# RWKV stage of a decoder trunk: block transposes on VectorE in place of DMAs through DRAM, mixes and masks on GpSimd, another order

## The chip, the cores and the metric

The kernel runs on one core of a Trainium2 chip. The metric is the device time of one execution in microseconds. The figure for the kernel before is the median of three runs. One further execution is recorded by the hardware profiler, and all durations below come from it. The engines are named as in the profile: PE is the tensor engine, DVE the vector engine, ACT the scalar engine, POOL is GpSimd, and SP is the engine that issues most DMAs.

## The reference

Two layers on a residual stream of 256 tokens by 1024 channels, all in float32. Each layer is SwiGLU, a token mixer, SwiGLU, each with a residual and a layer norm. The mixer of layer 0 is a spatial gating unit, that of layer 1 is RWKV-7 with 16 heads of 64. The change lies in the second mixer alone:

```python
xx = jnp.pad(x, ((0, 0), (1, 0), (0, 0)))[:, :-1] - x
x_rkv = x[None] + xx[None] * mu[:3, None, None, :]
r, k, v = jnp.einsum('nbsd,nde->nbse', x_rkv, w_rkv)
...
def step(state, inp):
    r_t, w_t, k_t, v_t, a_t, b_t = inp
    sa = jnp.einsum('bhij,bhj->bhi', state, a_t)
    state = (state * w_t[:, :, None, :] + sa[..., None] * b_t[:, :, None, :]
             + v_t[..., None] * k_t[:, :, None, :])
    y = jnp.einsum('bhij,bhj->bhi', state, r_t)
    return state, y
...
bonus = jnp.sum(r_h * k_h * r_k, axis=-1, keepdims=True) * v_h
out = ((y + bonus).reshape(bsz, seq, d).astype(x.dtype) * g) @ w_o
```

## The kernel before, in words

Tokens lie in two blocks of 128 (`m` = 0, 1). Weights come in units of 512 KB through four staging places (`Stream`): ACT rounds a unit (`wh`, L113), DVE takes the rest (`wl`, L114), and PE makes three one-pass products of them (L201 to L203). R and V of the RWKV stage use the units as they are (L281, `NATIVE`), a half of the depth at a time: `V101` is V, second half of the columns, block 0, second half of the depth.

The RWKV scan is done in chunks of 64 tokens. A chunk needs the inverse of a triangular 64x64 matrix per head. `ab` (L930) forms these matrices, 64 in all, each as two diagonal blocks of 32x32 and one block beside them. The 128 diagonal blocks are to be inverted with one block per partition, so `ab` writes them to DRAM (`dA`, on POOL's queue) and `inv_load` (L976) reads them back in the other layout. `inv_step` (L980) is 31 steps of two DVE instructions each. `inv_out` (L997) writes the result to DRAM (`dH`, `dG`) and reads it back on SP's queue as `G` and `Hf`. `offdiag` (`od`, `tp<-G,Aab`) and `offdiag2` (`oe`) are the products that complete the inverse, and `u` (L1108) is its first use in a chunk; `s` carries the state on, `x` and `rs` use it in the next chunk.

`mix_in` (L717) forms the inputs of R, K, V and of the gate, eight pieces of 128x128 a block on DVE (L714). `kprep` (`kp`) normalises the keys with a power on POOL (`rs`, L239). `decay_x` (`dc`) shifts the decays by one row with four DMAs a block (`Ex`), issued by ACT (`DX`). `rdone` (L852) makes four DVE instructions a half: the decayed `R`, and the bonus products and their sum. `scores` (`sc`) puts masks on the scores by DVE (`masked`). `stash` saves the residual through POOL's queue.

The order of PE's and SP's instructions is that of the program, and in this stage the string `ORDER` sets it, one token a step; the engine names in `ENG` are those that keep the program's order. For DVE and ACT (and for POOL before the change) a planner orders the instructions. Each engine and each DMA queue runs its instructions in the order in which they are given.

Of the kernel before, what the change touches and what calls it, by code (L numbers as in the profile page):

```python
# [11 lines left out]
F32 = mybir.dt.float32  # L12
# [8 lines left out]
ENG = {PE, SP}  # L21
# [33 lines left out]
class Stream:  # L55
    """Weight units in the order of their use: each is loaded ahead of time and split
    exactly into a rounded part and the rest, which one-pass products carry."""
# [12 lines left out]
    def free(self, now, v):  # L70
        """The next place of the ring for unit v, if the work issued up to op `now` is done with it."""
        shut = min((i for i in self.shut if i > now), default=1 << 30)
        n = N_W + (N_WX if self.ext and self.last[v] < shut else 0)
        for d in range(n):
            t = (self.turn + d) % n
            u = self.ring[t]
            if u is None or self.last[u] <= now:
                return t
        return None

    def load(self, now, upto=None):
        """Load what the staging places allow after the work issued up to op `now`."""
# [10 lines left out]
    def advance(self, now, ahead, upto=None):  # L93
        """Split the units that have a place, some ahead of use; `upto` must have one."""
# [29 lines left out]
class Builder:  # L124
# [14 lines left out]
    def extra(self, kind):  # L139
        """The room next to the lasting pools: more weight units, or more 4 KB tiles."""  # L140
# [77 lines left out]
    def to_cm(self, src):  # L218
        """[tokens, channels] -> rounded part and rest, [channel, block of channels, token]."""
# [52 lines left out]
    def proj(self, ps, m, xs, key, us):  # L272
        """ps[128 tokens, 512] += x[m] @ units us of key (two blocks of 128 rows each)."""
# [12 lines left out]
    def def_cols(self, key, src, cols):  # L286
        """Units of src[1024, columns]: 2 blocks of 128 rows by 512 columns each."""
# [16 lines left out]
    def proj_both(self, key, xs, done, between=None):  # L304
        """Both token blocks, two units at a time; between[i]: ops before the i-th quarter."""
# [317 lines left out]
    def rwkv(self, S):  # L623
        """The loads and the preparation that may come before the stage, and the stage."""
# [86 lines left out]
        def mix(n, m, q, out):  # L711
            for k in range(4 * q, 4 * q + 4):
                s = slice(k * P, k * P + P)
                V.scalar_tensor_tensor(out[:, s], st["xx"][m][:, s], st["mu"][:, n * 8 + k:n * 8 + k + 1],  # L714
                                       st["xf"][m][:, s], op0=ALU.mult, op1=ALU.add)
# [15 lines left out]
        def lora1(m):  # L731
            """The first products of both small nets, with a row of ones below for the second's bias."""
# [35 lines left out]
        def decay_x(m):  # L768
            """What stood before each token: the row above, or 1 at the start of a chunk."""
# [8 lines left out]
        def decay_w(m):  # L778
            """A chunk's last row is the decay of the whole chunk."""
# [131 lines left out]
        def cm_kb(m, i, q):  # L911
            """Chunk 0 has its keys before its b's, chunk 1 behind."""
# [43 lines left out]
        def scores(m, c, q):
            def f():
# [10 lines left out]
                for e in range(2):  # L968
                    masked(st["A"][ch][e][:, q * 512:q * 512 + 512], ps[e], self.mask)
# [6 lines left out]
        def inv_load():  # L976
            st["M"] = self.s4("M")
            DI.dma_start(st["M"], self.dA.rearrange("b s t -> b (s t)"))

        def inv_step(s):  # L980
            def f():
                if s == 0:
# [4 lines left out]
                V.tensor_tensor(tv, H3[:, 0:s + 1, s:s + 1].broadcast_to([P, s + 1, n]),  # L987
                                M3[:, s:s + 1, s + 1:32].broadcast_to([P, s + 1, n]), op=ALU.mult)
                V.tensor_tensor(hv, hv, tv, op=ALU.add)
            return f  # L990

        def inv_zero():
            st["Hf"] = [self.s4("Hf", x=True) for m in range(2)]
            for t in st["Hf"]:
                V.memset(t, 0.0)

        def inv_out():  # L997
            Mt, Ht = st["M"], st["H"]
# [6 lines left out]
            Gt = self.s4("G")
            st["G"] = Gt

            def back(m, blk, e):
                b0 = blk * 64 + e * 32 + m * 16
                r0 = e * 64 + blk * 32  # L1010
                q.dma_start(
                    Hf[m].rearrange("p (b t) -> p b t", t=64)[r0:r0 + 32, :, blk * 32:blk * 32 + 32],
                    self.dH[b0:b0 + 16].rearrange("b s t -> s b t"))

            for e in range(2):
                q.dma_start(Gt.rearrange("p (b t) -> p b t", t=32)[e * 64:e * 64 + 32],
# [352 lines left out]
```

## Time and profile before

| | |
|---|---|
| time, median of three runs | 1147.59 us (1144.7 to 1149.68) |
| the profiled execution, first to last instruction (span) | 1146.8 us |
| PE busy | 1103.2 us, 96% |
| DVE busy | 698.1 us, 61% |
| ACT busy | 481.2 us, 42% |
| POOL busy | 42.3 us, 4% |

Of the profiled execution the profile gives the span alone; the median of the runs is 0.8 us above it. A busy share of PE is no measure of its speed: its rows overlap, and while the granted clock is at the lower of its two levels (1.2 GHz, shown as 0.50; 2.4 GHz is shown as 1.00) it is as busy and does half as much. The RWKV stage lies between 724 and 946 us of the span.

### The profile page before, as it was taken

How to read it: one execution, taken by the hardware profiler on the slowest of the kernel's cores; microseconds unless marked ns; L12 is line 12 of the kernel's file. 1: busy time of each engine (PE TensorE's matmuls, PEld its weight loads, DVE VectorE, ACT ScalarE, POOL GpSimd, SP SyncE). 2: the span in 40 equal slices, each digit the busy share in tenths (PEclk: the TensorE clock that was granted, in tenths of full speed). 3: DMA queues.
4: the chain of work that ended last, by engine and by line, in shares of the span. 5: the costliest groups of instructions: out<-in, count | busy, mean ns of one | idle time of the engine just before them, and what ended most of it. 6: DMA issues, size and time to landing. Idle time of an engine off the chain costs nothing.

```text
span 1146.8 us, 15330 instructions
## 1 busy us (share of the span) xinstructions
PE 1103.2 (96%) x5854; PEld 878.3 (77%) x5854; DVE 698.1 (61%) x964; ACT 481.2 (42%) x632; POOL 42.3 (4%) x44
## 2 busy tenths in 40 slices
PE   7999999999999999999999999999989889999997
PEld 5788888778888888888788888775555768888885
DVE  5654556769658555457655453878655788555544
ACT  5544444455335444444444452462123145444430
POOL 0000000100000000000000000112100110000000
PEclk9999999999999999999999999999998999999999
DMA  8776565776644766655567563437876135766631
GB/s 277 244 236 187 182 196 168 233 254 201 215 147 151 243 204 199 187 184 154 189 218 224 184 199 125 165 93 251 269 203 222 60 123 190 245 201 196 184 111 37
DMA packets 153788, 216.51 MB, mean 189 GB/s; under 512 B 21197, under 2 KB 114829, under 8 KB 153714
## 3 DMA queue, kind: packets, MB, share of 16 engines
q1 hardware_dynamic: 152250, 210.80, 57.5%
q0 software_dynamic: 1024, 3.15, 1.0%
q10 hardware_dynamic: 440, 1.57, 0.5%
q8 instruction: 46, 0.75, 0.3%
q14 instruction: 28, 0.23, 0.1%
HBM read 209.46 MB, written 3.42 MB: 186 GB/s over the span
## 4 chain that ended last, share of the span: by engine, by line
PE 77%; DVE 8%; DMA 7%; issue 3%; ACT 2%; SPq 1%; POOL 1%; ACTq 0%; DVEq 0%; POOLq 0%
PE mm L201 14%; PE mm L203 14%; PE mm L202 14%; PE acc L201 8%; PE acc L203 8%; PE acc L202 8%; PE mm L281 3%; DMA raw<-ffn_w_in 3%; DVE wl L114 2%; PE tp L376 2%; ACT wh L113 1%; DMA raw<-sgu_w_in 1%; POOL rs L239 1%; SPq L90 1%; PE tp L215 1%
## 5 line engine op out<-in xcount | busy, mean ns | idle before, releaser
L114 DVE TENSOR_TENSOR wl<-raw,wh 128x1024 fp32r<-128x1024 f32 x328 | 396.2, 1221 | 272.7 <-ACT wh L113 264.7
L113 ACT CAST wh<-raw 128x1024 fp32r<-128x1024 f32 x328 | 340.4, 1051 | 347.7 <-PE acc L203 144.1
L201 PE MATMUL mm<-wh,xh 128*128 128x512 f32 x832 | 327.6, 394 | 8.3 <-DVE h L366 3.8
L202 PE MATMUL mm<-wl,xh 128*128 128x512 f32 x832 | 325.1, 391 | 1.2 <-DVE wl L114 1.2
L203 PE MATMUL mm<-wh,xl 128*128 128x512 f32 x832 | 325.1, 391 | 0.2 <-DVE xl L208 0.2
L201 PEld LDWEIGHTS mm<-wh,xh 128*128 128x128 f32 x832 | 156.6, 188 | 44.9 <-DVE h L366 5.5
L202 PEld LDWEIGHTS mm<-wl,xh 128*128 128x128 f32 x832 | 156.6, 188 | 34.8 <-DVE wl L114 3.2
L203 PEld LDWEIGHTS mm<-wh,xl 128*128 128x128 f32 x832 | 156.5, 188 | 34.4 <-DVE xl L208 1.9
L201 PE MATMUL acc<-wh,hT 128*128 128x512 f32 x352 | 140.9, 400 | 0.0
L203 PE MATMUL acc<-wh,hT 128*128 128x512 f32 x352 | 137.6, 391 | 0.0
L202 PE MATMUL acc<-wl,hT 128*128 128x512 f32 x352 | 137.2, 390 | 0.0
L365 ACT ACTIVATE h<-mm 128x256 f32<-128x256 f32 x88 | 33.8, 384 | 104.1 <-PE mm L203 104.1
L203 PEld LDWEIGHTS acc<-wh,hT 128*128 128x128 f32 x352 | 66.1, 188 | 14.3
L202 PEld LDWEIGHTS acc<-wl,hT 128*128 128x128 f32 x352 | 66.3, 188 | 12.8
L201 PEld LDWEIGHTS acc<-wh,hT 128*128 128x128 f32 x352 | 66.1, 188 | 12.5
L366 DVE TENSOR_TENSOR h<-h,mm 128x256 f32<-128x256 f32 x88 | 36.7, 417 | 58.8 <-ACT h L365 58.8
L281 PE MATMUL mm<-raw,mix 128*128 128x512 f32 x128 | 60.6, 619 | 0.7 <-DMA raw<-rwkv_w_rkv 0.7
L239 POOL TENSOR_TENSOR rs<-ve,mhalf 128x1 f32<-128x1 f32 x14 | 14.1, 1010 | 928.0 <-DVE ve L247 928.0
L281 PEld LDWEIGHTS mm<-raw,mix 128*128 128x128 f32 x128 | 24.0, 196 | 27.2 <-issue 25.1
L208 DVE TENSOR_TENSOR hT<-tp,hT 128x512 fp32r<-128x512 f32 x44 | 30.1, 684 | 7.6 <-ACT hT L207 7.6
L207 ACT CAST hT<-tp 128x512 fp32r<-128x512 f32 x44 | 25.8, 587 | 9.0 <-PE tp L376 8.9
L261 DVE SCALAR_TENSOR_TENSOR y<-acc,x 128x512 f32<-128x512 f32 x24 | 15.9, 685 | 18.7 <-PE acc L203 18.7
(189 smaller groups left out, 878.4 us busy)
## 6 DMA issues: line engine op xcount, KB each, us to landing
raw<-ffn_w_in SPq DMA_DIRECT2D x352, 256.0 KB, 3.9
raw<-ffn_w_out SPq DMA_DIRECT2D x88, 512.0 KB, 3.9
raw<-rwkv_w_rkv SPq DMA_DIRECT2D x40, 512.0 KB, 4.0
raw<-sgu_w_in SPq DMA_DIRECT2D x32, 512.0 KB, 4.9
raw<-sgu_w_out SPq DMA_DIRECT2D x16, 512.0 KB, 3.5
raw<-rwkv_w_o SPq DMA_DIRECT2D x8, 512.0 KB, 3.5
lng<-ln_g SPq DMA_DIRECT2D x6, 512.0 KB
lnb<-ln_b SPq DMA_DIRECT2D x6, 512.0 KB
```

The source lines that it names most:

```text
L113: nc.scalar.copy(h, raw)
L114: nc.vector.tensor_tensor(l, raw, h.bitcast(F32), op=ALU.subtract)
L201: i = mm(out, lhsT=lh, rhs=rh, start=start, stop=False)
L202: mm(out, lhsT=lh, rhs=rl, start=False, stop=False)
L203: mm(out, lhsT=ll, rhs=rh, start=False, stop=stop)
L207: self.nc.scalar.copy(h, src)
L208: self.nc.vector.tensor_tensor(l, src, h.bitcast(F32), op=ALU.subtract)
L239: self.nc.gpsimd.tensor_tensor(rs, v, self.mhalf[:, :w], op=ALU.pow)
L281: i = self.nc.tensor.matmul(ps, lhsT=xs[:, c], rhs=h[:, s], start=kk == 0, stop=kk == 7)
L365: nc.scalar.activation(hb[:, o + 256:o + 512], ps[:, 0:256], AF.Silu)
L366: nc.vector.tensor_tensor(hb[:, o:o + 256], hb[:, o + 256:o + 512], ps[:, 256:512], op=ALU.mult)
L376: nc.tensor.transpose(ps[:, o:o + P], st["h"][c][:, hh:hh + P], self.ident)
```

## The change

1. The inverse: `ab` masks the diagonal blocks and the block beside them into two tiles (`D`, `Aof`), ACT copies one half of the partitions of `Aof` into `D`, and `inv_load` is one DVE transpose of 32x32 blocks. `inv_out` is two such transposes (`G`, `Hd`). `inv_fill` (`hf`) copies `Hd` into `Hf` on POOL, four copies a block. `offdiag` and `offdiag2` use `accb` banks and share their copies out between ACT and DVE. The DRAM tiles `dA`, `dH`, `dG` are gone.
2. The mixes of R, V and the gate are two POOL instructions a half (12 halves, 24 instructions of 128x512). Those of K stay on DVE.
3. The bonus products: ACT copies the product, POOL multiplies twice, DVE sums when `R` is done. The masks of the scores of chunk 0: ACT copies, POOL masks. `Hf` is cleared by POOL.
4. `behind` fixes where some DVE instructions stand among the steps of the inverse.
5. POOL's order is that of the program (`ENG`); `DX` is SP; `ORDER` is another.

```diff
-ENG = {PE, SP}
+ENG = {PE, SP, mybir.EngineType.Pool}
...
         def mix(n, m, q, out):
+            if n != 1:
+                k3 = lambda t: t[:, half(q)].rearrange("p (k t) -> p k t", k=4)
+                mu = st["mu"][:, n * 8 + 4 * q:n * 8 + 4 * q + 4].unsqueeze(2).broadcast_to([P, 4, P])
+                G.tensor_tensor(k3(out), k3(st["xx"][m]), mu, op=ALU.mult)
+                G.tensor_tensor(out[:, half(q)], out[:, half(q)], st["xf"][m][:, half(q)], op=ALU.add)
+                return
...
-                V.tensor_tensor(R[:, s], ps, st["E"][m][0][:, s], op=ALU.mult)
-                V.tensor_tensor(rk, ps, st["kp"][m][:, s], op=ALU.mult)
-                V.tensor_tensor(rk, rk, st["r_k"][:, s], op=ALU.mult)
-                V.tensor_reduce(bo[:, h * 8:h * 8 + 8], heads(rk), axis=AX.X, op=ALU.add)
+                rk = st["rk", m][:, s]
+                behind(V.tensor_tensor(R[:, s], ps, st["E"][m][0][:, s], op=ALU.mult))
+                A.copy(rk, ps)
+                G.tensor_tensor(rk, rk, st["kp"][m][:, s], op=ALU.mult)
+                G.tensor_tensor(rk, rk, st["r_k"][:, s], op=ALU.mult)
...
+            if pool:
+                A.copy(out, ps)
+                o3 = out.rearrange("p (h t) -> p h t", t=n)
+                G.tensor_tensor(o3, o3, mask.unsqueeze(1).broadcast_to([P, 512 // n, n]), op=ALU.mult)
+                return
...
-                        DA.dma_start(self.dA[b0:b0 + 16].rearrange("b s t -> s b t"),
-                                    t3[r0:r0 + 32, :, blk * 32:blk * 32 + 32])
+                p3 = ps.rearrange("p (b t) -> p b t", b=8)
+                for out, k in ((Of, 32), (D, 0)):
+                    V.tensor_tensor(out.rearrange("p (b t) -> p b t", b=8), p3[:, :, k:k + 32],
+                                    self.mask[:, k:k + 32].unsqueeze(1).broadcast_to([P, 8, 32]), op=ALU.mult)
+                for e in range(2):
+                    r = slice(e * 64 + 32, e * 64 + 64)
+                    A.copy(D[r, :], Of[r, :])
...
-                    masked(st["A"][ch][e][:, q * 512:q * 512 + 512], ps[e], self.mask)
+                    masked(st["A"][ch][e][:, q * 512:q * 512 + 512], ps[e], self.mask, ch == 0)
...
-            DI.dma_start(st["M"], self.dA.rearrange("b s t -> b (s t)"))
+            V.transpose(st["M"].rearrange("p (s t) -> p t s", s=32), st["D"].rearrange("p (b t) -> p t b", b=32))
...
+        def behind(inst):
+
+            if st.get("step"):
+                self.after(inst, st["step"])
+                st["step"] = inst
...
-            q.dma_start(self.dH.rearrange("b s t -> b (s t)"), Ht)
-            V.tensor_copy(M3[0:64], H3[0:64].rearrange("p s t -> p t s"))
...
-            q.dma_start(self.dG.rearrange("b s t -> b (s t)"), Mt[0:64, :])
...
+            behind(V.transpose(st["G"].rearrange("p (b s) -> p s b", b=32), H.rearrange("p (s t) -> p t s", s=32)))
+            st["step"] = None
+            st["Hd"] = self.s4("Hd")
+            V.transpose(st["Hd"].rearrange("p (b t) -> p t b", b=32), H.rearrange("p (s t) -> p t s", s=32))
+
+        def inv_fill(m):
+            def f():
+                for blk in (1, 0):
...
+                        r = slice(e * 64 + blk * 32, e * 64 + blk * 32 + 32)
+                        out = st["Hf"][m].rearrange("p (b t) -> p b t", t=64)[r, :, blk * 32:blk * 32 + 32]
+                        src = st["Hd"][r, m * 512:m * 512 + 512].rearrange("p (b t) -> p b t", t=32)
+                        G.tensor_copy(out, src)
+            return f
...
-        DX, DW, DA, DI, DO = A, nc.sync, G, A, nc.sync
+        DX, DW = nc.sync, nc.sync
...
-p:k_k cm00 cm01 l1_0 lw00 mixK00 flush mixK01 K000 K001 cm10 cm11 la00 lw01 dec00 p:k_a dec01 dc0 mixK10 p:gn_g
...
+p:k_k cm00 cm01 l1_0 lw00 mixK00 flush mixK01 mixV00 mixV01 K000 K001 cm10 cm11 la00 lw01 dec00 p:k_a dec01 mixK10 mixR00 mixR01
...
```

What this makes of the queues is seen at three places. The first is POOL from the end of the layer norm before the stage (`rs<-ve`) to the keys' second power (`rs<-ss`); `mix_5861` and `mix_5991` are V's, `mix_5942` and `mix_5996` are R's, `mix_6070` is the gate's. Before:

```order
L239 TENSOR_TENSOR rs<-ve,mhalf 128x1
L890 DMA dX<-x_5853 128x1024
L239 TENSOR_TENSOR rs<-ss,mhalf 128x8 x4
L952 DMA dA<-Aab_6265 32x16x32 x4
L952 DMA dA<-Aab_6374 32x16x32 x4
```

Now, from the eighth mix instruction to the stash:

```order
L716 TENSOR_TENSOR mix_5942<-mix_5942,xf_5784 128x512
L715 TENSOR_TENSOR mix_5991<-xx_5896,muT 128x512
L716 TENSOR_TENSOR mix_5991<-mix_5991,xf_5895 128x512
...
L239 TENSOR_TENSOR rs<-ss,mhalf 128x8
L715 TENSOR_TENSOR mix_5996<-xx_5896,muT 128x512
L716 TENSOR_TENSOR mix_5996<-mix_5996,xf_5895 128x512
...
L239 TENSOR_TENSOR rs<-ss,mhalf 128x8
L898 DMA dX<-x_5713 128x1024
L898 DMA dX<-x_5850 128x1024
```

The four powers of the keys stood one behind the other with nothing between; now 14 mix instructions stand ahead of the first, 20 ahead of the second, and 24 and both stashes ahead of the third and fourth.

The second is DVE around the inverse, from the masks of the last `ab` product to the first step. Before, the steps of the inverse began behind a DMA (row L987 of the trace, `M` from `dA`), and at their end stood:

```order
L987 TENSOR_TENSOR T_6417<-H_6253,M_6415 128x31
L989 TENSOR_TENSOR H_6253<-H_6253,T_6417 128x31
L1002 COPY M_6415<-H_6253 64x1024
L927 TENSOR_TENSOR A_6636<-tp,mask 128x512
L927 TENSOR_TENSOR A_6637<-tp,mask 128x512
```

Now the start and the end of the same work read:

```order
L891 TENSOR_REDUCE bonus_6309<-rk_6310 128x8
L961 TENSOR_TENSOR Aof_6266<-tp,mask 128x256
L961 TENSOR_TENSOR D_6265<-tp,mask 128x256
L961 TENSOR_TENSOR Aof_6266<-tp,mask 128x256
L961 TENSOR_TENSOR D_6265<-tp,mask 128x256
L990 STREAM_TRANSPOSE M_6401<-D_6265 128x32x32
...
L1001 TENSOR_TENSOR H_6253<-H_6253,T_6403 128x31
L1019 STREAM_TRANSPOSE G_6638<-H_6253 128x32x32
L1022 STREAM_TRANSPOSE Hd_6640<-H_6253 128x32x32
L1048 COPY Q_6652<-acc 32x512 x2
```

The sum of the bonus (`L891`), which waits for POOL, stands ahead of the masks, and the transposes stand directly behind masks and steps.

The third is PE between the score product of chunk 0 and the state product of chunk 0 (`od` is L1032 before and L1043 now, `oe` is L1047 before and L1058 now, `u0` is L1108 before and L1120 now). Now:

```order
L281 MATMUL mm<-raw_6502,mix_5991 128x512 x2
L215 MATMUL tp<-ident,Em_6131 128x128 x4
L1151 MATMUL tp<-g_182_6247,mix_6115 128x160 x4
L1151 MATMUL tp<-g_183_6249,mix_6115 128x160 x4
L1156 MATMUL tp<-ident,gs_6624 128x128
L1157 MATMUL tp<-ident,gs_6624 32x128
L1043 MATMUL acc<-G_6638,Aof_6266 32x32 x64
...
L1058 MATMUL acc<-Hd_6640,Q_6652 32x32 x64
L978 MATMUL tp<-ZR_6139,KBT_6160 128x128 x8
L1120 MATMUL tp<-X,Hf_6562 64x64 x16
L978 MATMUL tp<-ZR_6140,KBT_6161 128x128 x8
```

Ahead of `od` stand six halves of R and V since the last `ab` product (R100, V100, V101, R101, V010, V011; eight before, and V100 stood ahead of `ab10`); between `od` and `oe` stands the first score product of the chunk (`av0`), and between `oe` and `u0` a block of scores.

## Rows read from the trace of the kernel before

**Rows 1.** The page: its first line and the busy time of each engine.

```profile
span 1146.8 us, 15330 instructions
PE 1103.2 (96%) x5854; PEld 878.3 (77%) x5854; DVE 698.1 (61%) x964; ACT 481.2 (42%) x632; POOL 42.3 (4%) x44
```

**Rows 2.** Who PE waited for, 724 to 946 us: in total, times, longest us.

```profile
PE tp L215 <- DVE o L1189: 3.9, 1, 3.9
PE tp L1032 <- DMA G<-dG: 1.8, 2, 1.4
PE tp L966 <- DVE VU L1113: 1.6, 1, 1.6
PE acc L752 <- ACT ah L743: 1.5, 1, 1.5
PE tp L1108 <- issue: 1.5, 1, 1.5
PE tp L215 <- DVE Aab L927: 1.1, 1, 1.1
PE tp L215 <- DVE a L828: 1.0, 1, 1.0
PE tp L215 <- DVE Ep L859: 0.8, 1, 0.8
PE tp L1159 <- DVE A L927: 0.8, 1, 0.8
PE mm L281 <- DMA raw<-rwkv_w_rkv: 0.7, 1, 0.7
```

**Rows 3.** Stretches of 5 us: busy time by engine, granted clock, DMA share, GB/s.

```profile
750.00:755.00 5.00, 4.38 (x11) 2.86 (x12) 3.97 (x11) 4.45 (x9) 0.00 (x0) 0.76 0.13 43
850.00:855.00 5.00, 3.25 (x73) 1.75 (x73) 2.50 (x4) 0.00 (x0) 0.00 (x0) 1.00 0.63 106
855.00:860.00 5.00, 4.67 (x183) 4.53 (x179) 0.96 (x2) 2.31 (x4) 0.00 (x0) 0.50 0.70 150
860.00:865.00 5.00, 3.54 (x58) 2.92 (x55) 1.80 (x4) 0.61 (x2) 0.00 (x0) 0.50 0.88 335
900.00:905.00 5.00, 3.38 (x44) 2.89 (x39) 3.97 (x9) 1.21 (x2) 2.58 (x2) 0.78 0.02 5
```

**Rows 4.** PE in order of time, 840 to 872 us: start, duration, line, operation.

```profile
848.28 3.70 PE L281 MATMUL mm<-raw,mix 128*128 128x512 f32 x8
864.24 5.88 PE L281 MATMUL mm<-raw,mix 128*128 128x512 f32 x8
```

**Rows 5.** ACT in order of time, at the keys of the second token block.

```profile
749.50 0.62 ACT L207 CAST mh<-mix 128x512 fp32r<-128x512 f32 x1 [2.61 <-DMA Ex<-Ep]
```

**Rows 6.** POOL in order of time, the whole span.

```profile
209.08 1.49 POOL L467 TENSOR_SCALAR_AFFINE_SELECT wsp<-wsp 128x1024 f32<-128x1024 f32 x1 [0.38 <-DMA wsp<-sgu_w_sp]
210.76 1.30 POOL L467 TENSOR_SCALAR_AFFINE_SELECT wsp<-wsp 128x1024 f32<-128x1024 f32 x1 [0.20 <-PE tp L215]
737.84 0.92 POOL L239 TENSOR_TENSOR rs<-ve,mhalf 128x1 f32<-128x1 f32 x1 [12.35 <-DVE ve L247]
740.64 0.58 POOL L890 DMA_DIRECT2D dX<-x  x1 [1.88 <-DVE x L253]
773.99 1.94 POOL L239 TENSOR_TENSOR rs<-ss,mhalf 128x8 f32<-128x8 f32 x1 [6.04 <-DVE ss L811]
```

**Rows 7.** Line 253 on DVE, 200 to 215 us: duration ns min/median/max.

```profile
L253 DVE SCALAR_TENSOR_TENSOR x<-y,rs,lnb x2: 747/1166/1584, 208.9 to 209.5; 128x512 f32<-128x512 f32 x2
```

**Rows 8.** DVE, 724 to 946 us: the mixes as a group, then the inverse in order of time.

```profile
L714 DVE SCALAR_TENSOR_TENSOR mix<-xx,muT,xf 128x128 f32<-128x128 f32 x64 | 17.6, 343 | 0.0
...
815.88 0.18 DVE L987 TENSOR_TENSOR T<-H,M 128x31 f32<-128x31 f32 x1
842.23 0.21 DVE L989 TENSOR_TENSOR H<-H,T 128x31 f32<-128x31 f32 x1
842.48 1.05 DVE L1002 COPY M<-H 64x1024 f32<-64x1024 f32 x1
```

More of the change, by code (lines that the diff above doesn't have):

```diff
@@ L711, in mix @@
         def mix(n, m, q, out):
+            if n != 1:
[4 more added lines that the diff above has]
+                return
             for k in range(4 * q, 4 * q + 4):
                 s = slice(k * P, k * P + P)
-                V.scalar_tensor_tensor(out[:, s], st["xx"][m][:, s], st["mu"][:, n * 8 + k:n * 8 + k + 1],
-                                       st["xf"][m][:, s], op0=ALU.mult, op1=ALU.add)
+                behind(V.scalar_tensor_tensor(out[:, s], st["xx"][m][:, s], st["mu"][:, n * 8 + k:n * 8 + k + 1],
+                                              st["xf"][m][:, s], op0=ALU.mult, op1=ALU.add))
         def mix_in(n, m, q):
@@ L883, in f @@
                 v, vb = st["v", m][:, half(n)], st["vb"][m][:, half(n)]
+                V.tensor_reduce(st["R"][m][1][:, n * 8:n * 8 + 8], heads(st["rk", m][:, half(n)]), axis=AX.X, op=ALU.add)
                 V.tensor_tensor(heads(vb), heads(v), per_head(st["R"][m][1][:, n * 8:n * 8 + 8], 8), op=ALU.mult)
@@ L923, in cm_kb, with masked @@
             return f
-        def masked(out, ps, mask):
+        def masked(out, ps, mask, pool=False):
             n = mask.shape[1]
-            V.tensor_tensor(out.rearrange("p (h t) -> p h t", t=n), ps.rearrange("p (h t) -> p h t", t=n),
-                            mask.unsqueeze(1).broadcast_to([P, 512 // n, n]), op=ALU.mult)
+            if pool:
[3 more added lines that the diff above has]
+                return
+            behind(V.tensor_tensor(out.rearrange("p (h t) -> p h t", t=n), ps.rearrange("p (h t) -> p h t", t=n),
+                                   mask.unsqueeze(1).broadcast_to([P, 512 // n, n]), op=ALU.mult))
         def ab(m, c):
             def f():
-                if c == 0:
-                    st["Aab", m] = self.s4("Aab")
-                t = st["Aab", m]
+                if c == 0 and m == 0:
+                    st["D"], st["Aof"] = self.s4("D"), self.s4("Aof")
+                b0 = (m * 16 + c * 8) * 32
+                D, Of = (st[k][:, b0:b0 + 256] for k in ("D", "Aof"))
                 ps = self.tpb()
@@ L994, in inv_zero @@
             for t in st["Hf"]:
-                V.memset(t, 0.0)
+                G.memset(t, 0.0)
         def inv_out():
-            Mt, Ht = st["M"], st["H"]
-            M3, H3 = (t.rearrange("p (s t) -> p s t", s=32) for t in (Mt, Ht))
-            q = DO
-            q.dma_start(self.dH.rearrange("b s t -> b (s t)"), Ht)
-            V.tensor_copy(M3[0:64], H3[0:64].rearrange("p s t -> p t s"))
-            Hf = st["Hf"]
-            q.dma_start(self.dG.rearrange("b s t -> b (s t)"), Mt[0:64, :])
[L1005 to L1016, printed above, removed]
-                            self.dG[e * 32:e * 32 + 32].rearrange("b s t -> s b t"))
-            for m in range(2):
-                for blk in range(2):
-                    for e in range(2):
-                        back(m, 1 - blk, e)
+            H = st["H"]
+            st["G"] = self.s4("G")
+            behind(V.transpose(st["G"].rearrange("p (b s) -> p s b", b=32), H.rearrange("p (s t) -> p s t", s=32)))
+            st["step"] = None
[4 more added lines that the diff above has]
+                for blk in (1, 0):
+                    for e in range(2):
+                        r = slice(e * 64 + blk * 32, e * 64 + blk * 32 + 32)
[3 more added lines that the diff above has]
+            return f
         def offdiag(m):
@@ L1036, in f @@
                     q0 = e * 64 + 32
-                    A.copy(Q[q0:q0 + 32, m * 512:m * 512 + 512], ps[q0:q0 + 32, :])
+                    (A.copy if e else V.tensor_copy)(Q[q0:q0 + 32, m * 512:m * 512 + 512], ps[q0:q0 + 32, :])
             return f
@@ L1051, in f @@
                     d0 = e * 64
-                    V.tensor_copy(st["Hf"][m].rearrange("p (b t) -> p b t", t=64)[d0:d0 + 32, :, 32:64],
-                                  ps[d0:d0 + 32, :].rearrange("p (b t) -> p b t", t=32))
+                    (A.copy if e else V.tensor_copy)(
+                        st["Hf"][m].rearrange("p (b t) -> p b t", t=64)[d0:d0 + 32, :, 32:64],
+                        ps[d0:d0 + 32, :].rearrange("p (b t) -> p b t", t=32))
             return f
```

43 lines of the change are left out of this document (16 added, 27 removed).

## The prediction

> **What bounds the kernel now.** I read the page first: PE is busy 96% of 1146.8 us [rows 1], so time can only come from PE waiting, or from PE running at its lower clock. Both lie close together. Before 724 us and after 946 us the diff touches nothing; between them lies the RWKV stage, and there the table of PE's waits is the view to read [rows 2]: the reader should see many short waits, no long one, and one family among them, the inverse. `od` waits 1.8 us for `G`, which comes back from DRAM, and `u0` (L1108) starts late by 1.5. Then the stretches [rows 3]: PE was busy only 3.25 of 5 us from 850 to 855, and from 855 to 865 its granted clock is 0.50, the 1.2 GHz level. One half of a projection on unsplit weights (eight instructions of L281) takes 5.88 us there against 3.70 before it [rows 4]. So the round trip costs more in clock than in waiting. A second place is ACT's queue: `mh` starts at 749.50 after 2.61 us behind the DMAs that ACT issued for `Ex` [rows 5]; PE waits 1.5 us for `ah` behind it [rows 2], and the clock of 750 to 755 is 0.76 [rows 3].
>
> **The change part by part.** PE has the same products in both kernels, in another order, so I add up waits and clock.
>
> *The inverse without DRAM.* Gone are the eight `dA` DMAs, `dH`, `dG`, and ten loads on SP, with the 1.8 and the 1.5 us. Half clock over 10 us costs PE 5.0 us at most, if all of it streams, and at least the 2.2 by which that half grew (5.88 - 3.70); I take 4.5, near the upper end, since those ten us are full of products. Together 7.8. The new `M`, `G` and `Hd` are three transposes; the nearest row is the strided copy it replaces, 1.05 us [rows 8], between 0.7 (plain reads) and 2.1 (twice as slow). They lie on DVE's chain.
>
> *`Ex` issued by SP.* ACT is free for `mh`: 1.5 us and 0.24 x 5 = 1.2 of clock, 2.7 together. The four DMAs of the second block now stand on SP ahead of the weights of the first R half, and wait there for the room of `x`, so for the stash that moved behind twenty mix instructions on POOL.
>
> *The new order.* `u2` is now followed by gate products, so the wait of 1.6 us for `VU` goes and with it 0.22 x 5 = 1.1 of clock (900 to 905): 2.7. The gate products no longer wait for a mask (0.8), the R transposes stand behind other work (0.8), and with the DRAM traffic of the inverse off SP I drop the wait for `raw` (0.7): 2.3. The last 3.9, for `o`, stays [rows 2].
> Gains: 7.8 + 2.7 + 2.7 + 2.3 = 15.5 us.
>
> *Mixes on POOL.* 48 of the 64 mix pieces leave DVE, 48 x 0.343 = 16.5 us [rows 8]. POOL gets 24 instructions of 128x512 with two inputs, each reading 1024 values per partition. No such row exists. The nearest that reads as much is the select, 1.30 and 1.49 us [rows 6]; above it I set 1.30 + 0.92 (the smallest two-input call) = 2.2, below it half a select, 0.65. I take 1.49, the select that ran beside DVE work. What counts is what stands behind them on POOL: the four `rs` of the keys, on which the transposes of `kk` and `a` hang. The third follows all 24, two other `rs` of 1.94 and two stash DMAs of 0.58; POOL is free at 737.84 + 0.92 = 738.8. It starts at 738.8 + 24p + 5.0 instead of 774.0, that is 24p - 30.2 late: 1.0 at 1.30, 5.6 at 1.49, 22.6 at 2.2. PE already loses 1.0 (`a`) and 1.1 (`Aab`) there [rows 2], so the cost is 5.6 - 2.1 = 3.5, from 0 to 20.5.
>
> DVE is held up as well: line 253 has two inputs in SBUF, and its second instance took 1.584 us in place of 0.747 [rows 7], while POOL ran the select of 209.08 [rows 6]: 0.84 us. If all 24 do that, DVE loses 20 us and is relieved of 16.5; its idle share (39% of the span, rows 1) covers the rest.
> The Trainium skill, page "SBUF — State Buffer", section "Who interferes with whom", says that a VectorE instruction with two SBUF inputs and a GpSimd instruction that reads SBUF exclude each other for the whole instruction, whichever came first. By that rule POOL, too, would wait for DVE each time, and the sum would be that of rival 3, 1153.0 in place of 1139.6. Line 253 agrees for DVE's side; for POOL's the two selects differ by 0.19 us only. The Trainium skill, page "GPSIMD Engine Reference", section "Elementwise — side-by-side cycle accounting", gives 4497 ns for a two-input instruction of 2048 values: an estimate of 1.12 us for 512, by which the mixes would cost nothing and the sum would be that of rival 1.
>
> *The inverse on DVE.* Its steps ran 26.6 us (815.88 to 842.44, rows 8) with six masks between them; now none, but the last half of R and its bonus sum stand between the steps. R's product is the fourth of six halves that PE does before `od`: 4 x 3.70 = 14.8, and DVE must wait for it there. With two transposes, 2.1, DVE is done some 29 to 33 us after the last mask. PE has six halves in that time, 22.2, and the small products among them. DVE's bonus sums (L891) wait for POOL's bonus products now; behind the first stand the masks of `ab10` and `ab11`, behind the second the last steps, and PE's `od` behind those. So `od` waits between 0 and 33 - 22.2 = 10.8 us; I take 2.0, near the low end, as scores, transposes and two gate stages fill most of it.
>
> *`u0`.* It now waits for eight copies on POOL (`hf0`, `hf1`) and for banks that DVE frees behind them. A copy has half the data of a select on a quarter of the partitions, 0.65 to 1.30: 5.2 to 10.4 from `Hd`. PE has `od`, `av0`, `oe` and a score block in front. Between 0 and 5; I take 2.0.
> Masks and bonus products on POOL follow the mixes and are due only after the inverse; ACT's extra copies fit its 42% [rows 1]. I cost them at nothing; the cover is POOL's time during the inverse, and if it is gone, `av0` is late.
>
> **Sum.** -15.5 + 3.5 + 2.0 + 2.0 = -8.0: a span of 1138.8. The median of the runs shown, 1147.59, is 0.8 above the profiled span, so I forecast 1139.6.
>
> **Rivals.**
> 1. *The mixes are free.* POOL takes 1.3 or less and the lock does not bite: -15.5 + 4.0 = -11.5, or 1136.1; without the two waits of 2.0, 1132.1. For it: in PE's queue V's and R's products stand behind all of the keys'. Against it: the 0.84 us of line 253. Chance 0.22.
> 2. *The clock stays low.* What follows the round trip are 128 products of 32x32 (`od`, `oe`), and the clock may fall for these and not for the wait: 4.5 stay, 1144.1, which is no change. Against it: PE waited just ahead of the fall [rows 3]. Chance 0.13.
> 3. *The lock alternates.* Each mix instruction waits for one DVE instruction, 1.30 + 0.75 = 2.05: 19.0 late, cost 16.9, so +5.4: 1153.0 (0.75 is line 253 undisturbed, rows 7). Against it: the select under DVE work took 0.19 more (1.49 against 1.30), not 0.75. Chance 0.13. It is the lock of the Trainium skill's page "SBUF — State Buffer".
> 4. *POOL is the bound, slower.* At 2.2 the third `rs` is 22.6 late, cost 20.5, so +9.0: 1156.6. It decides from 24p - 30.2 - 2.1 = 11.5, p = 1.83 us: above it the change loses, below it gains. PE would be seen waiting for `kk` and `a` between 755 and 800. Chance 0.14.
> The forecast has the rest, 0.38.
>
> **How the numbers follow.** 0.5%, 5.7 us, is about what a measurement of this kernel can tell from no change: faster is below 1141.9, slower above 1153.3. Faster: rival 1 and nearly all of the forecast, 0.58. Same: rival 2, most of rival 3 and the forecast's edge, 0.27. Slower: rival 4 and the rest of 3, 0.15. The range goes from 1129.5 (rival 1 with no new wait, all 5.0 of clock, and the waits of 1.0 and 1.1 gone too: 1132.1 - 0.5 - 2.1) to 1154, just past rival 3; it leaves out rival 4.
>
> **What would show it.** Right: no waits of PE for `G` by DMA, granted clock 1.0 in most of the stretch after `od`, mixes of about 1.5 us on POOL, the third `rs` some 5 us later against the keys than before. Wrong: mixes above 1.8 us; DVE's `kk` waiting for POOL over 3 us a time; a clock of 0.5 again at `od` and `u0`; PE's waits between 740 and 800 above 10 us in sum.

## The result: 3 per cent slower

The changed kernel takes 1180.9 us (median of 4 runs, 1176.95 to 1183.88), the kernel before 1147.06 on the same chip (median of 4): a ratio of 1.0296, with a 95% interval from 1.0271 to 1.0321. The forecast was 1139.6, in a range from 1129.5 to 1154. The profiled execution of the changed kernel:

```profile
span 1181.1 us, 15316 instructions
...
PE 1117.1 (95%) x5854; PEld 888.3 (75%) x5854; DVE 709.0 (60%) x908; ACT 488.8 (41%) x648; POOL 94.3 (8%) x82
```

PE's busy share is nearly that of before (95% against 96%, [rows 1]) in a span that is 34.3 us longer, so the table of PE's waits and the clock have to tell where those are. The waits of PE between 720 and 990 us (in total, times, longest):

```profile
PE acc L758 <- ACT ah L749: 7.4, 1, 7.4
PE mm L1094 <- DVE A L940: 5.8, 4, 3.9
PE tp L978 <- DVE S L1136: 4.4, 1, 4.4
PE tp L215 <- DVE o L1201: 3.9, 1, 3.9
PE mm L202 <- DVE wl L114: 3.3, 1, 3.3
PE tp L215 <- DVE a L834: 3.1, 1, 3.1
PE acc L1043 <- DVE G L1019: 2.9, 1, 2.9
```

These answer to [rows 2]. The wait for `G` by DMA is gone, that for `VU` fell from 1.6 to 0.7; the wait for `ah` went from 1.5 to 7.4, and three waits for DVE (`A`, `S`, `wl`) are new or longer. Some stretches (PE, PEld, DVE, ACT and POOL busy, granted clock, DMA share, GB/s), as in [rows 3]:

```profile
750.00:755.00 5.00, 0.06 (x1) 0.00 (x0) 5.00 (x6) 0.62 (x1) 4.76 (x6) 0.83 0.20 66
755.00:760.00 5.00, 2.50 (x3) 1.18 (x4) 2.64 (x4) 3.33 (x6) 1.20 (x1) 0.50 0.00 0
...
855.00:860.00 5.00, 5.00 (x152) 4.82 (x149) 1.37 (x2) 1.74 (x3) 4.53 (x8) 0.50 0.11 30
910.00:915.00 5.00, 1.15 (x26) 0.89 (x22) 5.00 (x7) 0.08 (x1) 1.26 (x1) 0.87 0.53 165
935.00:940.00 5.00, 3.59 (x32) 2.99 (x32) 3.84 (x7) 0.00 (x0) 1.40 (x1) 0.50 0.29 102
```

From 750 to 755 PE is idle but for 0.06 us, while DVE is busy all the time with six instructions; behind that the clock is at 0.50. It is at 0.50 again behind the inverse, where the change was to remove that, and at 935. What PE waits for at 750 is on ACT, which can round K's mix (`mh`) only when DVE has made it, and copies `ah` behind that:

```profile
756.38 0.62 ACT L207 CAST mh<-mix 128x512 fp32r<-128x512 f32 x1 [4.15 <-DVE mix L720]
...
757.18 0.26 ACT L749 COPY ah<-tp 64x128 f32<-64x128 f32 x1
```

To add this up for each run, I cut the stage, from 722 us on, at events that every kernel has (755 us, the last `ab` product, the first `od`, the first `u`, the last `y`, 28 us behind it). In steps of 1 us, PE's idle time is the step less PE's busy time, and its lost clock the busy time by one minus the granted clock; the two are added ("loss" below; the stretch from the first `u` to the last `y` is called the tail). The sums follow the spans to within some 4 us.

| kernel | to 755 | to `ab` | to `od` | to `u` | to `y` | behind | sum | span |
|---|---|---|---|---|---|---|---|---|
| before | 3.3 | 3.0 | 5.5 | 3.3 | 10.9 | 6.1 | 32.2 | 1146.8 |
| changed | 7.2 | 17.1 | 5.3 | 6.4 | 26.3 | 6.3 | 68.6 | 1181.1 |
| `mix_dve` | 1.4 | 7.8 | 5.3 | 5.7 | 28.6 | 7.0 | 55.8 | 1166.8 |
| `old_order` | 3.3 | 20.4 | 15.1 | 1.3 | 15.4 | 6.3 | 61.7 | 1175.3 |
| `old_order_mix` | 0.6 | 9.7 | 6.7 | 4.0 | 10.3 | 6.1 | 37.5 | 1150.7 |
| `inv_only` | 2.1 | 3.5 | 6.6 | 1.2 | 13.8 | 7.3 | 34.6 | 1148.6 |
| `inv_fill` | 2.1 | 5.8 | 8.8 | 2.1 | 6.5 | 6.6 | 31.9 | 1145.7 |
| `pool_only` | 2.0 | 9.1 | 5.1 | 2.9 | 10.7 | 7.5 | 37.2 | 1151.2 |
| `dx_sp` | 0.6 | 7.7 | 5.6 | 3.3 | 11.7 | 6.3 | 35.2 | 1147.1 |
| `tail` | 8.0 | 17.1 | 2.4 | 5.3 | 23.4 | 7.4 | 63.6 | 1176.2 |
| `tail_mix` | 1.4 | 8.2 | 2.4 | 5.2 | 22.5 | 7.4 | 47.0 | 1157.4 |
| `mix_later2` | 0.6 | 21.3 | 5.2 | 5.5 | 25.7 | 6.3 | 64.7 | 1176.7 |

The first two rows show two places: 18.0 us more up to the last `ab` (24.3 against 6.3), and 15.4 more between the first `u` and the last `y`. In the first, DVE's groups between 735 and 805 us (busy us, mean ns of one, idle before) show what is slow:

```profile
L720 DVE SCALAR_TENSOR_TENSOR mix<-xx,muT,xf 128x128 f32<-128x128 f32 x8 | 9.7, 1280 | 0.0
...
L820 DVE SCALAR_TENSOR_TENSOR kp<-sq,kp 128x512 f32<-128x512 f32 x4 | 5.4, 1350 | 0.0
...
L253 DVE SCALAR_TENSOR_TENSOR x<-y,rs,lnb 128x512 f32<-128x512 f32 x2 | 3.2, 1642 | 0.0
L800 DVE TENSOR_TENSOR kk<-mm,k_k 128x512 f32<-128x512 f32 x4 | 2.7, 682 | 1.1 <-PE mm L203 1.1
...
L816 DVE TENSOR_REDUCE ss<-sq 128x8 f32<-128x512 f32 x4 | 2.7, 680 | 5.9 <-ACT sq L814 5.9
```

K's mix takes 1280 ns a piece, where it took 343 before [rows 8]; line 253 took 747 where nothing ran beside it [rows 7] and takes 1642 here. Lines 800 (from PSUM) and 816 (a reduction of one input) take their usual 0.68. What runs beside them on POOL:

```profile
L716 POOL TENSOR_TENSOR mix<-mix,xf 128x512 f32<-128x512 f32 x12 | 18.7, 1559 | 0.9
L715 POOL TENSOR_TENSOR mix<-xx,muT 128x512 f32<-128x512 f32 x12 | 15.6, 1299 | 0.0
```

The mean of the 24 is 1.43 us (34.3 / 24), close to the 1.49 that the forecast took. And POOL does not hold the powers of the keys up, it waits for DVE (in the brackets: idle time before, and who ended it):

```profile
763.44 2.03 POOL L239 TENSOR_TENSOR rs<-ss,mhalf 128x8 f32<-128x8 f32 x1 [7.24 <-DVE ss L817]
...
780.94 2.03 POOL L239 TENSOR_TENSOR rs<-ss,mhalf 128x8 f32<-128x8 f32 x1 [4.86 <-DVE ss L817]
...
790.86 2.04 POOL L239 TENSOR_TENSOR rs<-ss,mhalf 128x8 f32<-128x8 f32 x1 [0.71 <-DVE ss L817]
```

### The profile page after: what moved, and what is told of

It reads as the page before. It is cut to its first block, busy times and chain, and to the rows that moved or that the text cites. A ratio compares the mean times of both kernels' runs of the same rounds, so it can differ in the third digit from the quotient of the medians.

```text
span 1181.1 us, 15316 instructions
## 1 busy us (share of the span) xinstructions
PE 1117.1 (95%) x5854; PEld 888.3 (75%) x5854; DVE 709.0 (60%) x908; ACT 488.8 (41%) x648; POOL 94.3 (8%) x82
## 4 chain that ended last, share of the span: by engine, by line
PE 79%; DVE 9%; DMA 5%; ACT 2%; issue 2%; POOL 1%; SPq 1%; DVEq 0%; ACTq 0%; POOLq 0%
PE mm L201 14%; PE mm L203 14%; PE mm L202 14%; PE acc L201 8%; PE acc L203 8%; PE acc L202 8%; PE mm L281 4%; DMA raw<-ffn_w_in 3%; DVE wl L114 2%; PE tp L376 1%; ACT wh L113 1%; DMA raw<-sgu_w_in 1%; POOL rs L239 1%; PE tp L215 1%; DVE mix L720 1%
```

## The experiments

**The mixes back on DVE (`mix_dve`).**

```diff
-            if n != 1:
+            if False:
```

> The changed kernel, with the mixes of R, V and the gate back on DVE in pieces of 128x128; all else as changed. Theory 1 (POOL's mixes and DVE's instructions with two SBUF inputs exclude each other, and that costs the keys' stage): the eight pieces of K's mix at 746 us, 9.71 us in the changed kernel, fall back to about 2.2; PE's idle time and lost clock between 723 and the last ab product, 24.3 us, falls to below 10; the time to 1163 to 1169 us. Rival (the keys are late by the new order, or by Ex on SP, and the mixes are only there at the same time): K's mixes or what stands ahead of them on DVE stay late, DVE gets 16.5 us more, and the time is 1178 us or more.

1167.61 us, ratio to before 1.0162 (1.0127 to 1.0196), against 1.0296 for the whole change: the mixes cost some 15 us (0.0134 x 1147). DVE between 735 and 760 us:

```profile
L720 DVE SCALAR_TENSOR_TENSOR mix<-xx,muT,xf 128x128 f32<-128x128 f32 x34 | 9.4, 345 | 0.0
...
L253 DVE SCALAR_TENSOR_TENSOR x<-y,rs,lnb 128x512 f32<-128x512 f32 x2 | 1.4, 743 | 0.0
```

The same line takes 345 ns again, and the loss up to `ab` falls from 24.3 to 9.2. That is as theory 1 has it: a DVE instruction with two inputs in SBUF is held up while POOL runs a mix (below, "the lock"). The loss behind `u` stays (28.6), so it has another cause.

**The order of before (`old_order`).** The order string of before, `hf0 hf1` behind `iout`, and `ENG` without POOL.

> The changed kernel with the order string of before (with the two copies of the diagonal blocks behind iout), and POOL's order left to the planner; mixes on POOL, block transposes, Ex on SP stay. Theory 2 (the tail from 905 to 953 us, where PE idles 13.3 and loses 8.1 us of clock, comes of the new order, which brings the bonus and normalisation work on DVE ahead of masks and of the state): the loss between the first u and the last y is 8 to 12 us as before, and the time 1160 to 1170 us. Rival (the tail comes of POOL's work and the lock, in whatever order): the loss stays above 20 us and the time above 1175 us.

1175.84 us, ratio 1.024 (1.021 to 1.027). The tail falls from 26.3 to 15.4, but 15.1 are lost ahead of `od` and 20.4 in the keys' stage. The 20.4 are where the lock works. The 15.1 are not the lock's: DVE idles there for 10.5 us (846 to 857), because `behind` holds the remaining steps of the inverse behind a mask that waits for PE. By its total the run speaks for the rival; by place the tail falls as theory 2 has it, if not as low, and the loss has come up elsewhere. `old_order_mix` below undoes both the mixes and `behind`.

**The block transposes alone (`inv_only`).** In the kernel before, only `ab`, `inv_load`, `inv_out`, `inv_fill` and the two `offdiag` are those of the change; the order string gets `hf0 hf1` behind `iout`.

> The kernel before with the block transposes alone: masks into D and Aof, three DVE transposes, the copies of Hd on POOL, offdiag in the other banks; its own order, mixes, bonus products and masks on DVE, Ex on ACT. Theory of the forecast: the wait for G and for u0 and the low clock behind them go, 5 to 8 us, 1139 to 1142 us. Rival (the transposes at 2 us each and the copies take the place of the round trip, and the clock falls all the same for the 32x32 products): within 3 us of before, 1144 to 1150 us.

1153.7 us, ratio 1.0047 (1.003 to 1.0063): slower, which neither theory said. The stretches of 2.5 us from `od` on (columns as above):

```profile
850.00:852.50 2.50, 2.50 (x84) 1.50 (x84) 0.00 (x0) 0.00 (x0) 2.30 (x5) 1.00 0.56 197
852.50:855.00 2.50, 2.13 (x131) 2.02 (x126) 2.18 (x4) 1.16 (x2) 1.44 (x3) 1.00 0.76 240
855.00:857.50 2.50, 1.50 (x70) 1.23 (x62) 2.47 (x5) 0.58 (x1) 0.00 (x0) 0.89 0.56 196
857.50:860.00 2.50, 1.99 (x30) 1.84 (x30) 0.49 (x1) 0.58 (x1) 0.00 (x0) 0.50 0.64 200
```

`od` and `oe` run at the full clock and u0 starts at 856.9 in place of 860.6. Then PE waits 0.9 us for `Hf` and some less for more of it, is busy 1.50 of 2.50, and the clock falls behind that. So the clock does not fall while the 32x32 products run. It falls behind them and behind a wait that is still there; which of the two brings it down, this run can't tell. Elsewhere time is lost: DVE's steps begin early and stand ahead of the evacuation of R, for which PE waits 2.4 us (0.8 before), and 2.0 for `X` behind `u0`. At the last `y` nothing is left of the 3.7 us (919.8 in both). The profiled execution was the fastest of ten (1150.34 to 1157.96), so a part of the 5 us is in no trace here.

**The mixes alone (`pool_only`).** The kernel before with the six lines of the change in `mix`.

> The kernel before with the mixes of R, V and the gate on POOL, two instructions a half, where its order has them; all else as before. Theory 1 (the lock): DVE's instructions beside them take up to 1.6 us longer each, in the keys' and ab's chain too; 5 to 15 us slower, 1152 to 1162 us. Rival (at 1.4 us an instruction POOL is fast enough, and DVE is relieved of 16.5 us): 1143 to 1148 us.

1153.29 us, ratio 1.0044 (1.0025 to 1.0062): slower by some 5 us, at the lower end of theory 1. PE waits 6.6 us for `a` (line 834), 1.0 before [rows 2]. Alone, the mixes cost a third of what they cost in the changed kernel: there 4 mix instructions stand ahead of the first power of the keys on POOL, in the changed kernel 14, and K's pieces run undisturbed behind those 4. But one DVE instruction beside those 4 (739.6 to 744.1 us) shows that the lock can hold for more than one instruction of POOL; without the mixes it takes 0.68 us:

```profile
740.43 4.20 DVE L703 TENSOR_TENSOR xx<-xf 128x508 f32<-128x508 f32 x1 [1.14 <-ACT xf L699]
```

Nor is the price low for the old order as such: up to `ab`, `old_order` loses 23.7 us and `old_order_mix`, with the mixes on DVE, 10.3, a difference near the 15 us of the new order.

**The lock by itself (`lock_probe`).**

> Leaves the whole computation out: POOL's two mix instructions alone, DVE's alone, and POOL's beside DVE instructions of six kinds, one kind after the other. Theory 1 (one instruction at a time, if DVE reads two inputs from SBUF): DVE's 128x128 with two SBUF inputs takes 1.1 to 1.4 us beside the mixes against 0.34 alone, its 128x512 1.6 to 2.2 against 0.69, and POOL's mixes grow by about 0.3 and 0.7 us each; DVE with an input in PSUM, with one input and its transposes, and ACT, are undisturbed. Rival (the bandwidth of the memory is shared): all kinds get slower by a similar share, the instructions with one input too, and POOL's mixes by 10 to 30% beside any of them.

The groups of the one execution, as line, engine, operation, count, then busy us and mean ns. Lines 87 to 94 are alone, 98 to 132 beside one another: 98 to 101 DVE 128x128, 105 to 108 DVE 128x512, 115 an input in PSUM, 122 and 124 one input, 132 beside POOL's copies of 32x512; 143 transposes alone, 149 beside mixes.

```profile
L108 DVE TENSOR_TENSOR do<-xa,xb 128x512 f32<-128x512 f32 x8 | 11.4, 1420 | 0.2
L149 DVE STREAM_TRANSPOSE do<-xa 128x1024 f32<-128x1024 f32 x5 | 10.2, 2039 | 0.1
L101 DVE SCALAR_TENSOR_TENSOR do<-xa,xb 128x128 f32<-128x128 f32 x8 | 8.7, 1082 | 0.2
L115 DVE TENSOR_TENSOR do<-ps,xb 128x512 f32<-128x512 f32 x12 | 8.3, 690 | 0.4
...
L124 DVE COPY do<-xa 128x512 f32<-128x512 f32 x6 | 6.5, 1092 | 0.2
L132 DVE SCALAR_TENSOR_TENSOR do<-xa,xb 128x128 f32<-128x128 f32 x12 | 6.4, 531 | 0.4
L106 POOL TENSOR_TENSOR go<-go,xa 128x512 f32<-128x512 f32 x4 | 6.4, 1588 | 0.3
...
L105 POOL TENSOR_TENSOR go<-gi,xb 128x512 f32<-128x512 f32 x4 | 5.1, 1285 | 0.2
...
L99 POOL TENSOR_TENSOR go<-go,xa 128x512 f32<-128x512 f32 x4 | 5.0, 1262 | 0.3
...
L98 POOL TENSOR_TENSOR go<-gi,xb 128x512 f32<-128x512 f32 x4 | 4.2, 1040 | 0.2
L94 DVE TENSOR_TENSOR do<-xa,xb 128x512 f32<-128x512 f32 x6 | 4.2, 692 | 0.2
L122 DVE TENSOR_REDUCE do<-xa 128x8 f32<-128x512 f32 x6 | 4.1, 685 | 0.2
L143 DVE STREAM_TRANSPOSE do<-xa 128x1024 f32<-128x1024 f32 x2 | 4.0, 1977 | 0.0
...
L88 POOL TENSOR_TENSOR go<-go,xa 128x512 f32<-128x512 f32 x3 | 3.8, 1262 | 0.2
...
L87 POOL TENSOR_TENSOR go<-gi,xb 128x512 f32<-128x512 f32 x3 | 3.1, 1040 | 0.2
...
L92 DVE SCALAR_TENSOR_TENSOR do<-xa,xb 128x128 f32<-128x128 f32 x6 | 2.1, 351 | 0.2
...
L68 DVE COPY do<-xb 128x1024 f32<-128x1024 f32 x1 | 0.7, 694 | 5.3 <-DMA xb<-x 5.3
```

DVE's instruction with two inputs in SBUF takes 1082 ns in place of 351, and 1420 in place of 692; from PSUM 690, the reduction 685 and the transpose 2039 (1977 alone) are not held up. POOL's pair takes 1040 and 1262 alone and beside the short ones, 1285 and 1588 beside those of 128x512. That is theory 1 by kind, but for one point: the plain copy with one input is held up too (1092 ns for 512 values, 694 for 1024 without POOL). In size it is less than "one instruction at a time": 1420 lies under the range given, POOL pays nothing for a short DVE instruction and 0.25 and 0.33 us for a long one in place of 0.7, and eight long instructions of DVE and eight of POOL, 14.7 us by their times alone (8 x 0.692 + 4 x 1.040 + 4 x 1.262), took 12.7 side by side (32.0 to 44.7 us). Shared bandwidth, the rival, would have slowed the reduction. The Trainium skill, page "SBUF — State Buffer", section "Who interferes with whom", says that a VectorE instruction with two SBUF inputs contends with a GpSimd instruction that reads SBUF, that a copy can, and that a reduction never does on trn2; the kinds agree with these rows.

**Ex on SP alone (`dx_sp`).**

```diff
-        DX, DW, DA, DI, DO = A, nc.sync, G, A, nc.sync
+        DX, DW, DA, DI, DO = nc.sync, nc.sync, G, A, nc.sync
```

> The kernel before, with the DMAs of Ex issued by SP and nothing else. Forecast's term: 1.5 us of PE's wait for ah and 1.2 us of clock go, 2.7 us faster: 1144 to 1146.5 us where before is near 1148. Rival (SP's queue holds the weights up behind the wait for Ep, or the time goes to the next wait): no change within 1 us, or slower.

1148.68 us, ratio 1.0012 (0.9997 to 1.0027): no change. Up to 755 us the 2.7 us are gained exactly (3.3 to 0.6), and up to `ab` 4.7 are lost again: PE waits 2.9 us for `wl`, which DVE now has behind the keys' preparation. A wait was moved.

**Three moves in the new order (`tail`, `tail_mix`).**

```diff
-hf0 hf1 od0 od1 av0 oe0 oe1 sc010 x0 u0 sc011 V110 kb0
+hf0 hf1 V110 od0 od1 av0 oe0 bo00 oe1 bo01 sc010 x0 u0 sc011 kb0
...
-sc100 y1 bo00 bo01 cR11
+sc100 y1 cR11
...
-sc110 on00 on01 og00 y2 bo10 s2 un0 sc111 av3
+sc110 sc111 on00 on01 og00 y2 bo10 s2 un0 av3
```

The lines are shown in part; `p:gn_b`, which `bo00` needs, moves forward too. In both, `VU` of chunk 1 is copied from the tile with the bonus in it, which changes what is computed and not the instructions.

> The changed kernel with three moves in its order string: the bonus of block 0 (bo00, bo01, with gn_b) goes from behind y1 to between the offdiag products, where DVE idles; V110 goes from behind u0 to ahead of od0, where PE waits 2.9 us for G; sc111 goes from behind s2 to ahead of it. Theory 2, sharper (the tail is lost because DVE's and PE's work of the new order stands in the wrong place): PE's idle time and lost clock from the first u to the last y, 26.3 us, fall by 8 to 15, the 6.4 between od and u by 2 to 4, and the time to 1163 to 1171 us. Rival (the chain of the chunks itself is that long once everything is late): less than 4 us gained, above 1176 us.

> The same three moves in the order, in the kernel with the mixes back on DVE (mix_dve, 1167.6 us). Theories 1 and 2 as separate causes that add up: 1150 to 1158 us. Rival (both cure the same lateness): the moves give less than 4 us here, above 1163 us.

`tail` takes 1175.72 us (1.0249, from 1.0226 to 1.0272), `tail_mix` 1160.47 (1.0114, from 1.009 to 1.0138): about 5 us less than the whole change and than `mix_dve` (1.0296 - 1.0249, 1.0162 - 1.0114). The wait for `G` is filled (5.3 to 2.4 ahead of `od`), and the tail falls by 2.9 and 6.1. That is between theory and rival: these places are a part of the order's price, not all of it. Part of the gain was lost at once: with the wait for `G` filled, PE stops in the middle of `oe` for about as long, 2.8 us in `tail` and 2.5 in `tail_mix`, where the profile names nothing that it waited for (`issue`):

```profile
PE acc L1058 <- issue: 2.8, 1, 2.8
```

In `tail_mix` the sum of both causes came out, but 2.5 us above the range given.

**Mixes and order undone together (`old_order_mix`).** `old_order` with `if False` in `mix` and `behind` without effect.

> The changed kernel with two things undone at once: the mixes on DVE again, and the order string of before (hf0, hf1 behind iout; POOL left to the planner, and no fixed places for DVE's instructions among the steps). What stays of the change: block transposes, Ex on SP, masks of chunk 0 and bonus products on POOL and ACT. If the lock and the order are the two causes of the 33 us, this is as fast as the block transposes alone: 1149 to 1156 us. Rival (the masks and bonus products on POOL and ACT, or Ex on SP, carry a third share): above 1160 us.

1155.27 us, ratio 1.0076 (1.0049 to 1.0102). With the mixes on DVE, the new order, with the fixed places of `behind`, costs 1.0162 - 1.0076, some 10 us, and without them the tail is 10.3, as before. Ex, masks and bonus products add some 3 us to the transposes alone (1.0076 - 1.0047), where the intervals overlap.

**A half ahead of `u0` (`inv_fill`).**

```diff
-i4 cR01 i5 st0 mixG11 mixV11 V010 cK00 sc000
+i4 i5 st0 mixG11 mixV11 V010 cK00 cR01 sc000
...
-bo01 u0 gb R011 s0 R110 cR10
+bo01 R011 u0 gb R110 s0 cR10
```

> The block transposes alone (inv_only, 1153.7 us), with two moves in the old order: the R half R011 goes ahead of u0, R110 ahead of s0, so that PE has a half to do while Hf is copied; and cR01, which waited 2.4 us for DVE behind the steps, goes behind V010. Theory (what follows a wait of PE is about 10 us of the 1.2 GHz level, so a filled wait gives its clock back): the loss from od to u0 and behind it falls by 3 to 5 us and that ahead of od by 2: 1147 to 1150 us. Rival (the chain behind, VU and S on ACT and DVE, sets the end): no gain, 1152 to 1155 us.

1146.94 us, ratio 1.0 (0.9979 to 1.0021), the fastest version with the transposes: 5 us under `inv_only`, as fast as before. The gain is behind `u`, 13.8 to 6.5; the other move failed, since the wait for R's evacuation only moved on (8.8 ahead of `od`).

**Mixes that start later (`mix_later`, `mix_later2`).** POOL reads the factors from `muP`, a copy that DVE makes behind K's pieces.

```diff
+            if (m, q) == (1, 1):
+                st["muP"] = self.small("muP", [P, 48])
+                self.after(V.tensor_copy(st["muP"], st["mu"]), last)
```

> The changed kernel, but POOL's mixes read their factors from a copy that DVE makes behind the eight pieces of K's mix of block 0, so that they start after these. Theory 1 (K's mix is where the lock costs PE most, as it stands on the way to ah): the pieces take 0.34 us again, PE's wait of 7.4 us for ah falls below 2, and the lock moves on to the keys' preparation; 1170 to 1177 us. Rival (the lock costs the same wherever it falls): 1179 us or more.

> As mix_later, but the copy stands behind K's pieces of block 1, which are the eight at 746 us (those of block 0 had run before 737, so that mix_later delayed nothing); in the order, the mixes on POOL go behind mixK11. Theory 1 (a mix on POOL costs by the DVE instruction that it holds up, and K's pieces stand on the way to ah): these take 0.34 us each, the loss of PE up to 755 us falls from 7.2 to 1 to 2.5, and the lock and POOL's queue move on to the keys' preparation, which gives part of it back: 1172 to 1179 us. Rival (the lateness of ah comes from L253 and L703 to L708 ahead of the pieces, or from ACT): the loss up to 755 us stays above 5 us.

`mix_later` (with `(0, 1)` there) takes 1180.85 us (1.0299, from 1.0273 to 1.0325): my edit waited for the wrong block, and nothing moved. `mix_later2` takes 1179.28 (1.028, from 1.0263 to 1.0297), just above theory 1's range. The loss up to 755 us is 0.6 in place of 7.2, so K's pieces were what made `ah` late. Up to `ab` it is 21.3 in place of 17.1:

```profile
PE mm L202 <- DVE wl L114: 12.4, 1, 12.4
...
PE tp L215 <- DVE a L838: 4.2, 1, 4.2
```

The power of the keys now stands behind the mixes on POOL (it starts at 764.91, its input is there from 752.9), and DVE's `wl`, behind what waits for that power, takes 2.1 us a piece. Here POOL's queue does hold the keys up, as the forecast had it. Started 7 us later, the 24 instructions cost nearly the same.

## Why the prediction was wrong

- **The mixes: the step that failed.** The price of one, 1.49 us, was right (1.43). The cost was put at 3.5 us, by what stands behind them on POOL, and for DVE the prediction said that its idle share of 39% covers what it loses. It does not: from 745 to 755 DVE was busy throughout, K's mix stood on the way to `ah`, and its eight pieces took 9.7 us in place of 2.2. The third power was 16.9 us late (790.86 against [rows 6]), but POOL was idle ahead of it: DVE was late, not POOL. Measured, some 15 us. Row 253, read for its 0.84 us, had shown the lock; its price was laid against an average.
- **Rivals 3 and 4** were the nearest, with 0.27 together. Rival 4's bound, POOL at over 1.83 us, is not what happened. Rival 3 had the lock, but on POOL, where it costs about 0.3 us a time (1299 and 1559 ns against 1040 and 1262 alone), and not on DVE, where a piece of K's mix lost 0.9 us and L703 in `pool_only` 3.5. The rule of the Trainium skill's page "SBUF — State Buffer", section "Who interferes with whom", that the prediction cited was borne out by kind, and for DVE; POOL's loss of about 0.3 us is less than the 0.68 us of one DVE instruction.
- **The new order** was entered as a gain of 5.0 us (2.7 + 2.3). It costs some 10 with the mixes on DVE, `behind` included. Most of the waits named did go (`VU` fell from 1.6 to 0.7), but bonus sums, the splits of the weights of the next product and the masks now meet on DVE: from 910 to 915 it is busy for 5.00 us and PE for 1.15. The prediction had looked at the waits that go and not at which of DVE's work would be late next. Masks and bonus products on POOL, put at nothing, come with `Ex` to some 3 us, where the intervals overlap. Which single move carries the rest (`tail_mix` still loses 22.5) stays open.
- **The inverse without DRAM**, -7.8. The trip did go. In the changed kernel `od` waits 2.9 us for `G` (forecast 2.0) and the clock is at 0.50 all the same; alone, the transposes made the kernel some 5 us slower. The low clock was real, but it did not belong to that trip alone: it comes without the trip too, and with a half of R put ahead of `u0` the stretches from `od` to `y` lose 8.6 in `inv_fill` against 15.0 in `inv_only`. The early steps took DVE from R's evacuation. And the 1.5 us read as a late `u0` were misread: [rows 2] puts them down to `issue`, a stop inside `u0` for which the profile names no cause. Such stops, of 2.3 to 2.8 us, also stand in `oe` in `old_order_mix`, `tail` and `tail_mix`, which make no trip through DRAM, so they were not shown to be the trip's. What causes them stays open.
- **Rival 2**, that the clock falls for the 32x32 products, is not what happened in the changed kernel: there it falls between 852 and 853 us, while PE waits for `G`, and the first of these products starts at 853.17. In `old_order` it had fallen long before `od`, behind an idle stretch of 5.5 us, and is full again while `od` runs; but behind `oe`, with a wait of 0.9 us for `Hf`, it falls once more (2.5 us stretches, columns as above):

```profile
862.50:865.00 2.50, 0.00 (x0) 0.00 (x0) 2.29 (x7) 0.00 (x0) 0.00 (x0) 0.74 0.95 349
877.50:880.00 2.50, 2.50 (x87) 1.53 (x87) 0.09 (x1) 0.00 (x0) 1.76 (x3) 1.00 0.71 215
885.00:887.50 2.50, 2.16 (x31) 1.85 (x31) 0.44 (x1) 0.58 (x1) 0.00 (x0) 0.50 0.17 59
```

In `inv_fill`, where PE's longest wait between `od` and `u0` is 0.37 us, it still falls behind `oe`, to 0.50 from 861 to 864 us, while a wait of 0.7 us at 874 is followed by no fall:

```profile
857.50:860.00 2.50, 2.13 (x132) 2.02 (x126) 2.17 (x4) 1.15 (x2) 0.00 (x0) 1.00 0.73 231
860.00:862.50 2.50, 2.50 (x70) 1.92 (x63) 2.47 (x5) 0.58 (x1) 0.00 (x0) 0.61 0.03 7
862.50:865.00 2.50, 2.50 (x6) 1.01 (x5) 0.49 (x1) 0.58 (x1) 0.00 (x0) 0.71 0.03 7
```

So for the fall behind `oe` the rival is not refuted: whether the products or the short waits bring it about stays open.

- **`Ex` on SP**, -2.7: in `dx_sp` right for the two terms named, and given back in the next 50 us. Net nothing.
- **`u0`**, 2.0: PE waited 0.9 for the mask ahead of it; the copies on POOL were not late.

From the transposes alone, each step adds to the ratio: 1.0047, with `Ex`, masks and bonus products 1.0076, with the order 1.0162, with the mixes 1.0296. In us, that is 5.4 where the forecast had -3.8 (-7.8 + 2.0 + 2.0), 3.3 where it had -2.7, 9.9 where it had -5.0, and 15.4 where it had 3.5. The parts act on each other (with the mixes on POOL and `behind` kept, the order string is 1.0296 - 1.024, some 6 us), so these shares hold for this sequence.

## What to carry to other kernels

Before moving elementwise work to GpSimd, list what VectorE does in that stretch with two inputs from SBUF, or copies, and lay one GpSimd instruction's length against each: what counts is whether those stand on the bottleneck's path there, not VectorE's share of the whole span. When a wait is removed, name the next one and give the bottleneck work for it; here a stop of PE was often followed by a stretch at the lower clock as well. Undo the parts one by one: here a part that gained in its own place, `Ex` on SP, moved the end by nothing.

## What the hardware showed unexpectedly

A copy of one input (128x512) was held up by POOL too, 1092 ns, about as long as the short instruction with two (1082). Short DVE instructions (128x128) cost POOL nothing, 1040 and 1262 ns in either case, while each took 0.73 us longer on DVE (1082 against 351 ns). A DVE transpose of 128x1024 takes 1.9 to 2.1 us, twice the strided copy of 64x1024 [rows 8], the upper end of what was allowed for, and is not held up by POOL.
